# A bank for each half of the last accumulator, an earlier low part of the bias table, and weight splits that start one block later

## The chip, the cores and the metric

The kernel runs on one core of a Trainium2 chip. The metric is the device time of one execution in microseconds (us); the median of three runs of the kernel before is 1035.03 us. The core has a matrix engine (PE, whose weight loads the profile lists as PEld), a vector engine (DVE), a scalar engine (ACT), a general engine (POOL) and a queue engine (SP) that issues most transfers. Matmuls write their sums to PSUM, a memory of eight banks; a bank holds 512 float32 values in each of 128 partitions.

## The reference

One decoder layer for 256 tokens with 2048 features, in float32:

```
proj = x @ w_in                     # 16 latent queries, shared kv latent, gates, indexer, RG-LRU input
score = sum_h w_h * relu(q_idx_h . k_idx)        # causal, top 64 keys of each query
logits = q_lat . c_kv * scale + rel_bias[t5_bucket(t - s)]    # masked to the chosen keys
attn = softmax(logits) @ c_kv, up-projected per head, times silu(attn_gate), @ w_branch_a
h = RG-LRU(conv4(x_rnn)), times silu(rnn_gate), @ w_branch_b
merged = sigmoid(g_a) * attn_branch + sigmoid(g_b) * rnn_branch
out = layernorm(alpha * x + merged @ w_out) * ln_g + ln_b
```

## The kernel before, in words

Every weight is read once from memory, in pieces of 128x1024 float32 that the program numbers in the order of use. A piece lands in one of four `raw` buffers. ACT rounds it to a high part (`hi`, `hi_of`, line 97), DVE forms the low part (`lo`, `lo_of`, line 101) as raw minus hi, and PE multiplies with both, so that the sum has nearly float32 accuracy. There are five buffers for `hi` and five for `lo`. `split_to(n)` issues the split of all pieces up to n, `load_to(n)` their loads on SP.

The order of work on each engine is that in which the Python code records it; each engine takes its own instructions strictly in that order, and semaphores join the engines. The work has three stages that the change touches.

*The blocks* (lines 246 to 275). For k = 0 to 15, one block of x and one block of `wA` (kv latent, indexer key, half of the indexer queries) is split into `xs`, `ahi`, `alo` (three buffers each for `ahi` and `alo`), and PE adds 14 matmuls to six accumulators: `psc` (lines 266 to 268) and `psq` (line 204). In iteration k the split of block k + 1 is recorded first, then the matmuls of block k, and from k = 12 on one split of the main stream of weights (pieces 0 to 3).

*The main stream* (lines 779 to 818). Column jobs (`qi`, `ag`, `q`, `ga`, ...) follow each other on PE. Time is counted in ticks; a tick is one quarter of a small job's matmuls (8 of them). Side work is written as Python generators in an agenda: `spawn(t, gen)` starts one at tick t, and a `yield n` inside it puts its next step n ticks later. `post_a` evacuates `psc` at tick 0 and transposes the indexer key on PE (`psk`, line 333) at tick 3. `post_qi` evacuates `psq`. `scores(i)`, spawned at tick 13 + 4i, multiplies the indexer queries with the keys into two PSUM banks (`pss`, lines 379 and 381), reads them with ACT one tick later (lines 386, 387) and with DVE two ticks later (line 390). `rel`, spawned at tick 25, builds the table of relative position bias: high and low part of `rel_bias` in `rb`, then a matmul with a one-hot matrix (`psrel`, line 434) at tick 33. The tiles `psq`, `psk`, `pss` and `psrel` all come from four PSUM banks that are taken in turn (`aux_tile`): a new tile takes the bank of the fourth tile before it, once that tile's last reader is done. `scores(5)` takes two banks at tick 33 just ahead of `psrel`, and so `psrel` takes the bank of `pss4_0`, whose last reader is line 390 of `scores(4)`, recorded at tick 31.

*The last column chunk* (lines 891 to 905). The output projection's last 512 columns are done for one half of the tokens (t = 0) and then for the other (t = 1). For t = 1 they are cut in two halves of 256 columns, each 48 matmuls (lines 774 to 776). `residual` (lines 828, 829) adds alpha times x and takes the statistics of a finished half; `normalise(t)` forms mean and root, and for each 512 columns two DVE instructions, centre (line 851) and finish (line 854), and a store (line 855 on SP; the columns 1024 to 1535 go over ACT and POOL, lines 860 to 870). `normalise(0)` is recorded ahead of the first `residual` of t = 1. The accumulators come from four other banks, again in turn (`acc_tile`).

Of the kernel before, what the change touches and what calls it, by code (L numbers as in the profile page):

```python
# [73 lines left out]
def layer(ctx, tc, ar, out):  # L74
# [7 lines left out]
    def pool(name, side=None, **kw):  # L82
        return tc.tile_pool(name=name, bufs=1, side=side, **kw)
# [12 lines left out]
    def hi_of(hi, src):  # L96
        nc.scalar.activation(hi, src, AF.Copy)  # L97

    def lo_of(lo, src, hi):

        nc.vector.tensor_sub(lo, src, f(hi))  # L101

    def acc_tile(name):
        return psum.tile([P, 512], F32, name=name, tag="acc", bufs=4)

    def aux_tile(name):
        return psum.tile([P, 512], F32, name=name, tag="aux", bufs=4)

    def slot(name, dt=F32R):
        return big.tile([P, 2 * T], dt, name=name, tag="slot", bufs=16)  # L110
# [13 lines left out]
    def tick(t):  # L124
        for gen in agenda.pop(t, []):
            try:
                wait = next(gen)
            except StopIteration:
                continue
            spawn(t + (wait or 1), gen)  # L130
# [35 lines left out]
    def load_to(n):  # L166
        while st["load"] < min(n, len(halves)):
            i = st["load"]
            kind, a, s = halves[i]
            raw = wpool.tile([P, 1024], F32, name=f"raw{i}", tag="raw", bufs=4)  # L170
            if kind == "wt":
                src = ar["wt"][a, :, s * 8:(s + 1) * 8, :].rearrange("p k c -> p (k c)")
            else:
                src = ar[kind][a, s].rearrange("p k c -> p (k c)")
            nc.sync.dma_start(raw, src)
            raws[i] = raw
            st["load"] += 1

    def split_to(n):
        while st["split"] < min(n, len(halves)):  # L180
            i = st["split"]
            load_to(i + 1)
            raw = raws.pop(i)
            if NO + 24 <= i < NO + 28:
                pieces = []
                for e in range(2):
                    hi, lo = slot(f"wh{i}_{e}"), slot(f"wl{i}_{e}")
                    c = raw[:, e * 512:(e + 1) * 512]
                    hi_of(hi, c)
                    lo_of(lo, c, hi)  # L190
                    pieces.append((hi, lo))
                parts[i] = pieces
            else:
                hi = wpool.tile([P, 1024], F32R, name=f"hi{i}", tag="hi", bufs=5)
                lo = wpool.tile([P, 1024], F32R, name=f"lo{i}", tag="lo", bufs=5)
                hi_of(hi, raw)
                lo_of(lo, raw, hi)
                parts[i] = (hi, lo)
            st["split"] += 1

    def mm(ps, w, rhs, high, start, stop):

        n = 2 * T if high else T
        nc.tensor.matmul(ps[:, :n], w, rhs[:, :n], start=start, stop=stop)  # L204
# [16 lines left out]
    with pool("pha", side="right") as pha:  # L221
        ins = {}

        def load_a(k):
            xr = pha.tile([P, T], F32, name=f"xr{k}", tag="xr", bufs=4)
            nc.sync.dma_start(xr, ar["xT"][k])
            wr = pha.tile([P, NA], F32, name=f"wr{k}", tag="wr", bufs=4)
            if k == 0:
                nc.scalar.dma_start(wr[:, :A_Q], ar["wA"][k][:, :A_Q])
                nc.sync.dma_start(wr[:, A_Q:], ar["wA"][k][:, A_Q:])  # L230
            else:
                nc.sync.dma_start(wr, ar["wA"][k])
            ins[k] = (xr, wr)

        def split_a(k):
            xr, wr = ins.pop(k)
            hi_of(xs[:, k, :T], xr)
            lo_of(xs[:, k, T:], xr, xs[:, k, :T])
            hi = pha.tile([P, NA], F32R, name=f"ahi{k}", tag="ahi", bufs=3)
            lo = pha.tile([P, NA], F32R, name=f"alo{k}", tag="alo", bufs=3)  # L240
            for c in ([slice(0, A_Q), slice(A_Q, NA)] if k < 3 else [slice(0, NA)]):
                hi_of(hi[:, c], wr[:, c])
                lo_of(lo[:, c], wr[:, c], hi[:, c])
            return hi, lo

        for k in range(4):
            load_a(k)
        smalls = [(params, ar["params"]), (causal, ar["causal"]), (kvg, ar["kvg"].to_broadcast([P, DL])),
                  (relb, ar["relb"])]
        sp = {0: split_a(0)}  # L250
        for k in range(KT):
            if k + 1 < KT:
                sp[k + 1] = split_a(k + 1)
            if k + 4 < KT:
                load_a(k + 4)
            else:
                load_to(st["load"] + 1)
            if 8 <= k < 12:
                nc.sync.dma_start(*smalls[k - 8])
            hi, lo = sp.pop(k)  # L260
            fl = (k == 0, k == KT - 1)
            for t in range(2):
                o = psc[t][:, :A_Q]
                x_hi = xs[:, k, t * P:(t + 1) * P]
                x_lo = xs[:, k, T + t * P:T + (t + 1) * P]
                nc.tensor.matmul(o, x_hi, hi[:, :A_Q], start=fl[0], stop=False)
                nc.tensor.matmul(o, x_hi, lo[:, :A_Q], start=False, stop=False)
                nc.tensor.matmul(o, x_lo, hi[:, :A_Q], start=False, stop=fl[1])
            last = k == KT - 1
            for high in (False, True) if last else (True, False):  # L270
                for i in range(4):
                    w = (hi if high else lo)[:, A_Q + i * P:A_Q + (i + 1) * P]
                    mm(psq[i], w, xs[:, k, :], high, fl[0] and high, last and high)
            if k >= 12:
                split_to(k - 11)

    def evac(ps, name, dst=None):

# [145 lines left out]
    def rel():  # L424
        oh = idx.tile([32, VL], F32R, name="oh")
        nc.gpsimd.dma_start(oh, ar["onehot"])
        rb = idx.tile([32, 2, NH], F32R, name="rb")
        hi_of(rb[:, 0, :], relb)
        yield 6
        lo_of(rb[:, 1, :], relb, rb[:, 0, :])  # L430
        yield 2
        ps = aux_tile("psrel")
        for e in range(2):
            nc.tensor.matmul(ps[:NH, :], rb[:, e, :], oh, start=e == 0, stop=e == 1)
        yield
        v = idx.tile([NH, VL], F32, name="vrel")
        nc.scalar.activation(v, ps[:NH, :], AF.Copy, scale=DL ** 0.5)
        yield
        nc.gpsimd.dma_start(dv, v)
        for g in range(NH // HG):  # L440
            nc.gpsimd.dma_start(dz[g], bass.AP(tensor=dv.tensor, offset=dv.offset + g * SLAB,
                                               ap=[[0, P], [1, SLAB]]).rearrange("p (h v) -> p h v", h=HG))
            yield 10
# [303 lines left out]
    for i in range(4):  # L747
        spawn(1 + i, post_qi(i, psq[i]))
    spawn(25, rel())
    spawn(D0 + 20, lru_consts())  # L750
    for i in range(8):
# [17 lines left out]
    def products(o, w, i, d, xd, t, c=slice(0, 512)):  # L769

        hi, lo = (p[:, c] for p in (w[i] if isinstance(w, list) else [p[:, i * 512:(i + 1) * 512] for p in w]))
        mh = xd[:, t * P:(t + 1) * P]
        ml = xd[:, T + t * P:T + (t + 1) * P]
        nc.tensor.matmul(o, mh, hi, start=d == 0, stop=False)  # L774
        nc.tensor.matmul(o, mh, lo, start=False, stop=False)  # L775
        nc.tensor.matmul(o, ml, hi, start=False, stop=d == KT - 1)  # L776


    for kind, i in jobs:
        rhs = us if kind in ("ba", "bb") else {k: xs[:, k, :] for k in range(KT)}  # L780
        chunk = kind in CHUNKS
        ps = [acc_tile(f"ps_{kind}{i}_{t}") for t in range(2)] if chunk else acc_tile(f"ps_{kind}{i}")
        for qt in range(ticks((kind, i))):
            t = at[kind, i] + qt
# [12 lines left out]
            if t == FIN:  # L797
                dec_stack.close()
                fin = ctx.enter_context(pool("fin", side="right"))
                y = [fin.tile([P, DM], F32, name=f"y{e}") for e in range(2)]  # L800
# [5 lines left out]
            else:  # L806
                high = qt in (0, 3)
                w = parts[t // 2][0 if high else 1]
                for kk in range(8):
                    k = qt // 2 * 8 + kk  # L810
# [27 lines left out]
    rows = []  # L838
# [52 lines left out]
    last = range(NO + 24, NO + 32)  # L891
    cuts = [[slice(0, 512)], [slice(0, 256), slice(256, 512)]]
    for t in range(2):
        ps = acc_tile(f"psz{t}")
        for e, c in enumerate(cuts[t]):
            for n in last:
                for i in range(2):
                    d = 2 * (n - NO - 24) + i
                    products(ps[:, c], parts[n], i, d, xs[:, d, :], t, c)
                tick(t0)  # L900
                t0 += 1
                split_to(len(halves))
            residual(t, slice(3 * 512 + c.start, 3 * 512 + c.stop), 3 + e, ps[:, c])
        rows[-len(cuts[t]):] = [(t, slice(3 * 512, 4 * 512), ps if t else y[t][:, 3 * 512:])]
        normalise(t, 3 + len(cuts[t]))
    assert not agenda, agenda

# [51 lines left out]
```

## Time and profile before

| | |
|---|---|
| median of three runs (lowest, highest) | 1035.03 us (1034.36, 1035.72) |
| the profiled execution | 1034.45 us |
| its span, first to last instruction | 1032.7 us |
| PE busy | 1015.0 us, 98% of the span |
| PE weight loads busy | 881.0 us, 85% |
| DVE, ACT, POOL busy | 678.8 us (66%), 551.6 us (53%), 82.0 us (8%) |
| chain that ended last | PE 96%, DVE 2%, DMA 1% |
| mean granted PE clock | 0.995 of full |

A row of a timeline gives the start and length of an instruction (or of several alike, with their count), its engine, line and operation, the tile written and the tiles read, and in brackets how long the engine had sat idle before and what, by the profile, ended that. A matmul's length includes the time through the array, so that starts of neighbours lie closer together than a length.

### The profile page before, as it was taken

Reading aid. Unit: us, or ns where it says so; the run is one execution under the profiler, and the core shown is the slowest. Engines: PE = TensorE matmul, PEld = TensorE weight load, DVE = VectorE, ACT = ScalarE, POOL = GpSimd, SP = SyncE. Lnnn points to the kernel's source line nnn. Section 1 sums busy time; section 2 is a strip of 40 time slices with the busy share of each in tenths; the row PEclk is TensorE's granted clock in tenths of the full one; section 3 lists DMA queues with packets and bytes.
Section 4 is the critical chain, followed back from the end, with each engine's and each line's share of the span. In section 5 each row is a group of like instructions: output and inputs, shape, how many; then the busy total and the mean of one; then the engine's idle time right before and its main releaser. Section 6 shows DMA issues by size and latency. Waiting matters only on the chain.

```text
span 1032.7 us, 14867 instructions
## 1 busy us (share of the span) xinstructions
PE 1015.0 (98%) x5464; PEld 881.0 (85%) x5464; DVE 678.8 (66%) x1147; ACT 551.6 (53%) x910; POOL 82.0 (8%) x120
## 2 busy tenths in 40 slices
PE   9999999999999999999999999999999999999994
PEld 8888888998999988888888888888888888888884
DVE  6668775677677766544454888855577875566565
ACT  6666654555555565444334566588655554444431
POOL 0004312001111100000000000000500000000002
PEclk9999999999999999999999999999999999999997
DMA  9745877656566565665667666556666678666632
GB/s 306 265 144 171 276 252 233 194 171 178 170 189 174 183 184 162 185 191 196 192 196 213 196 186 194 171 183 190 193 190 185 200 252 283 186 192 190 186 120 82
DMA packets 61000, 201.41 MB, mean 195 GB/s; under 512 B 6608, under 2 KB 13136, under 8 KB 59904
## 3 DMA queue, kind: packets, MB, share of 16 engines
q1 hardware_dynamic: 59264, 191.29, 60.1%
q0 software_dynamic: 1232, 8.49, 2.1%
q8 instruction: 43, 0.70, 0.3%
q10 hardware_dynamic: 432, 0.70, 0.2%
q14 instruction: 29, 0.24, 0.1%
HBM read 198.31 MB, written 6.32 MB: 198 GB/s over the span
## 4 chain that ended last, share of the span: by engine, by line
PE 96%; DVE 2%; DMA 1%; issue 0%; ACT 0%; SPq 0%; DVEq 0%; ACTq 0%
PE ps_q L204 17%; PE ps_ag L204 9%; PE ps_rg L204 9%; PE ps_xr L204 9%; PE ps_ga L776 3%; PE ps_bb L776 3%; PE ps_gb L776 3%; PE ps_gb L775 3%; PE ps_ga L774 3%; PE ps_bb L774 3%; PE ps_ba L776 3%; PE ps_ba L774 3%; PE ps_bb L775 3%; PE ps_ga L775 3%; PE ps_gb L774 3%; PE ps_ba L775 3%
## 5 line engine op out<-in xcount | busy, mean ns | idle before, releaser
L101 DVE TENSOR_TENSOR lo<-raw,hi 128x1024 fp32r<-128x1024 f32 x324 | 399.5, 1234 | 307.1 <-ACT hi L97 303.3
L97 ACT ACTIVATE hi<-raw 128x1024 fp32r<-128x1024 f32 x324 | 341.5, 1054 | 175.6 <-PE ps_ba L776 52.6
L204 PE MATMUL ps_q<-xs,hi 128*128 128x512 f32 x512 | 122.4, 391 | 0.0
L204 PEld LDWEIGHTS ps_q<-xs,hi 128*128 128x128 f32 x512 | 94.0, 188 | 18.3
L204 PE MATMUL ps_q<-xs,lo 128*128 128x256 f32 x512 | 71.2, 283 | 0.0
L204 PEld LDWEIGHTS ps_q<-xs,lo 128*128 128x128 f32 x512 | 66.3, 190 | 1.4
L204 PE MATMUL ps_ag<-xs,hi 128*128 128x512 f32 x256 | 61.2, 391 | 0.0
L204 PE MATMUL ps_rg<-xs,hi 128*128 128x512 f32 x256 | 61.2, 391 | 0.0
L204 PE MATMUL ps_xr<-xs,hi 128*128 128x512 f32 x256 | 61.2, 391 | 0.0
L204 PEld LDWEIGHTS ps_rg<-xs,hi 128*128 128x128 f32 x256 | 47.1, 188 | 9.1
L204 PEld LDWEIGHTS ps_ag<-xs,hi 128*128 128x128 f32 x256 | 47.1, 188 | 9.1
L204 PEld LDWEIGHTS ps_xr<-xs,hi 128*128 128x128 f32 x256 | 47.0, 188 | 9.1
L774 PE MATMUL ps_bb<-hi,ub 128*128 128x512 f32 x128 | 50.4, 393 | 0.0
L774 PE MATMUL ps_ga<-hi,xs 128*128 128x512 f32 x128 | 50.0, 391 | 0.0
L776 PE MATMUL ps_bb<-hi,ub 128*128 128x512 f32 x128 | 49.9, 390 | 0.0
L776 PE MATMUL ps_ga<-hi,xs 128*128 128x512 f32 x128 | 49.9, 390 | 0.0
L776 PE MATMUL ps_gb<-hi,xs 128*128 128x512 f32 x128 | 49.9, 390 | 0.0
L775 PE MATMUL ps_gb<-lo,xs 128*128 128x512 f32 x128 | 49.8, 389 | 0.0
L775 PE MATMUL ps_ga<-lo,xs 128*128 128x512 f32 x128 | 49.8, 389 | 0.0
L775 PE MATMUL ps_bb<-lo,ub 128*128 128x512 f32 x128 | 49.8, 389 | 0.0
L774 PE MATMUL ps_ba<-hi,ua 128*128 128x512 f32 x128 | 49.8, 389 | 0.0
L775 PE MATMUL ps_ba<-lo,ua 128*128 128x512 f32 x128 | 49.8, 389 | 0.0
(273 smaller groups left out, 1888.7 us busy)
## 6 DMA issues: line engine op xcount, KB each, us to landing
raw<-in_wt SPq DMA_DIRECT2D x168, 512.0 KB, 4.2
raw<-in_wga SPq DMA_DIRECT2D x32, 512.0 KB, 3.6
raw<-in_wba SPq DMA_DIRECT2D x32, 512.0 KB, 3.5
raw<-in_wgb SPq DMA_DIRECT2D x32, 512.0 KB, 3.5
raw<-in_wbb SPq DMA_DIRECT2D x32, 512.0 KB, 3.7
raw<-in_wo SPq DMA_DIRECT2D x32, 512.0 KB, 3.6
wr<-in_wA SPq DMA_DIRECT2D x15, 424.0 KB, 4.6
dz<-dv POOLq DMA_DIRECT2D x4, 1024.0 KB, 8.6
```

The source lines that it names most:

```text
L97: nc.scalar.activation(hi, src, AF.Copy)
L101: nc.vector.tensor_sub(lo, src, f(hi))
L204: nc.tensor.matmul(ps[:, :n], w, rhs[:, :n], start=start, stop=stop)
L774: nc.tensor.matmul(o, mh, hi, start=d == 0, stop=False)
L775: nc.tensor.matmul(o, mh, lo, start=False, stop=False)
L776: nc.tensor.matmul(o, ml, hi, start=False, stop=d == KT - 1)
```

## The change

Three edits. The last accumulator of t = 1 becomes two tiles, one per half, and the line that joined the two halves for `normalise` goes, so that centre, finish and store are done per half of 256 columns. In `rel` the low part of `rb` is recorded at tick 28 where it was at tick 31; the matmul stays at tick 33. In the blocks, the splits of pieces 0, 1 and 2 are recorded in iterations 13, 14 and 15 where they were in 12, 13 and 14, and the split of piece 3 moves out of the blocks to tick 0 of the main stream, where `split_to(5)` issues it together with piece 4.

```diff
-            if k >= 12:
-                split_to(k - 11)
+            if k >= 13:
+                split_to(k - 12)
...
         hi_of(rb[:, 0, :], relb)
-        yield 6
+        yield 3
         lo_of(rb[:, 1, :], relb, rb[:, 0, :])
-        yield 2
+        yield 5
...
     for t in range(2):
-        ps = acc_tile(f"psz{t}")
         for e, c in enumerate(cuts[t]):
+            ps = acc_tile(f"psz{t}_{e}")
             for n in last:
...
             residual(t, slice(3 * 512 + c.start, 3 * 512 + c.stop), 3 + e, ps[:, c])
-        rows[-len(cuts[t]):] = [(t, slice(3 * 512, 4 * 512), ps if t else y[t][:, 3 * 512:])]
         normalise(t, 3 + len(cuts[t]))
```

ACT at the end of the blocks, before: `ahi` is a block's high part, `hi` a piece of the main stream, `pa0` the evacuated `psc`.

```order
L97 ACTIVATE ahi13_464<-wr13_395 128x848
L97 ACTIVATE hi0_484<-raw0_468 128x1024
L97 ACTIVATE xs_93<-xr14_418 128x256
L97 ACTIVATE ahi14_490<-wr14_420 128x848
L97 ACTIVATE hi1_510<-raw1_494 128x1024
L97 ACTIVATE xs_93<-xr15_443 128x256
L97 ACTIVATE ahi15_516<-wr15_445 128x848
L97 ACTIVATE hi2_536<-raw2_520 128x1024
L97 ACTIVATE hi3_556<-raw3_540 128x1024
L323 ACTIVATE pa0_585<-psc0_132 128x336
L97 ACTIVATE hi4_593<-raw4_591 128x1024
```

The same place in the changed kernel:

```order
L97 ACTIVATE ahi13_464<-wr13_395 128x848
L97 ACTIVATE xs_93<-xr14_418 128x256
L97 ACTIVATE ahi14_486<-wr14_420 128x848
L97 ACTIVATE hi0_506<-raw0_468 128x1024
L97 ACTIVATE xs_93<-xr15_443 128x256
L97 ACTIVATE ahi15_512<-wr15_445 128x848
L97 ACTIVATE hi1_532<-raw1_490 128x1024
L97 ACTIVATE hi2_552<-raw2_516 128x1024
L323 ACTIVATE pa0_581<-psc0_132 128x336
L97 ACTIVATE hi3_587<-raw3_536 128x1024
L97 ACTIVATE hi4_593<-raw4_591 128x1024
```

Block 14 now stands ahead of piece 0, and piece 3 behind `pa0`; the low parts stand on DVE in the same new order.

DVE around the low part of `rb`, before, with `lo18` to `lo20` pieces of the main stream and `rl4_0`, `rl4_1` the reads of `pss4_0` and `pss4_1`:

```order
L101 TENSOR_TENSOR lo18_1107<-raw18_959,hi18_1106 128x1024
L400 SCALAR_TENSOR_TENSOR score0_568<-rl3_0_1066,wi_567,score0_568 128x128
L400 SCALAR_TENSOR_TENSOR score1_569<-rl3_0_1066,wi_567,score1_569 128x256
L284 TENSOR_TENSOR s_ag2_1130<-ps_ag2_1015,r_ag2_1104 128x256
L400 SCALAR_TENSOR_TENSOR score0_568<-rl3_1_1069,wi_567,score0_568 128x128
L400 SCALAR_TENSOR_TENSOR score1_569<-rl3_1_1069,wi_567,score1_569 128x256
L101 TENSOR_TENSOR lo19_1150<-raw19_1002,hi19_1149 128x1024
L101 TENSOR_TENSOR rb_1044<-relb_90,rb_1044 32x16
L390 TENSOR_TENSOR rl4_0_1140<-pss4_0_1120,rl4_0_1140 128x128
```

The same place in the changed kernel:

```order
L101 TENSOR_TENSOR rb_1044<-relb_90,rb_1044 32x16
L101 TENSOR_TENSOR lo18_1108<-raw18_959,hi18_1107 128x1024
L400 SCALAR_TENSOR_TENSOR score0_564<-rl3_0_1066,wi_563,score0_564 128x128
L400 SCALAR_TENSOR_TENSOR score1_565<-rl3_0_1066,wi_563,score1_565 128x256
L284 TENSOR_TENSOR s_ag2_1131<-ps_ag2_1015,r_ag2_1105 128x256
L400 SCALAR_TENSOR_TENSOR score0_564<-rl3_1_1069,wi_563,score0_564 128x128
L400 SCALAR_TENSOR_TENSOR score1_565<-rl3_1_1069,wi_563,score1_565 128x256
L101 TENSOR_TENSOR lo19_1151<-raw19_1002,hi19_1150 128x1024
L390 TENSOR_TENSOR rl4_0_1141<-pss4_0_1121,rl4_0_1141 128x128
```

Only `rb` has moved; `lo19` and the read of `pss4_0` follow each other as before.

PE between the two halves of the last accumulator, before; a row names the engine whose semaphore it waits for:

```order
L775 MATMUL psz1_9810<-lo327_9725,xs_93 128x256
L776 MATMUL psz1_9810<-hi327_9724,xs_93 128x256
L774 MATMUL psz1_9810<-wh320_0_9624,xs_93 128x256 [waits DVE_49]
L775 MATMUL psz1_9810<-wl320_0_9625,xs_93 128x256
L776 MATMUL psz1_9810<-wh320_0_9624,xs_93 128x256
```

The same place in the changed kernel:

```order
L775 MATMUL psz1_0_9810<-lo327_9725,xs_93 128x256
L776 MATMUL psz1_0_9810<-hi327_9724,xs_93 128x256
L774 MATMUL psz1_1_9861<-wh320_0_9624,xs_93 128x256
L775 MATMUL psz1_1_9861<-wl320_0_9625,xs_93 128x256
L776 MATMUL psz1_1_9861<-wh320_0_9624,xs_93 128x256
```

The second half has a tile of its own and its first matmul has no wait for DVE.

## Rows read from the trace of the kernel before

**Rows 1.** Waits of PE in the whole span: us in total, times, longest
```profile
PE psz L774 <- DVE st L829: 4.8, 1, 4.8
PE psrel L434 <- ACT hi L97: 1.3, 1, 1.3
...
PE psc L267 <- DVE alo L101: 0.4, 1, 0.4
```

**Rows 2.** Timeline, the two halves of the last accumulator: start us, us, engine
```profile
1010.03 0.28 PE L776 MATMUL psz<-hi,xs 128*128 128x256 f32 x1
...
1014.67 0.43 DVE L829 BATCH_NORM_STATS2 st<-psz 128x6 f32<-128x256 f32 x1
...
1015.16 0.39 PE L774 MATMUL psz<-wh,xs 128*128 128x256 f32 x1 [4.85 <-DVE st L829]
...
1022.38 0.28 PE L776 MATMUL psz<-hi,xs 128*128 128x256 f32 x1
1022.70 0.43 DVE L828 SCALAR_TENSOR_TENSOR psz<-y,psz 128x256 f32<-128x256 f32 x1 [7.59 <-PE psz L776]
```

**Rows 3.** Stretches there: length, busy us (count) PE, PEld, DVE, ACT, POOL, clock, DMA
```profile
1004.40:1010.30 5.90, 5.90 (x49) 5.70 (x47) 4.70 (x10) 2.48 (x4) 1.29 (x1) 1.00 0.01 3
...
1015.10:1018.70 3.60, 3.54 (x18) 3.54 (x19) 0.01 (x1) 0.00 (x0) 0.00 (x0) 0.56 0.19 73
```

**Rows 4.** Timeline, the last instruction on DVE and the last store
```profile
1028.39 0.75 DVE L854 SCALAR_TENSOR_TENSOR y<-psz,lt,gb 128x512 f32<-128x512 f32 x1
1029.17 0.33 SPq L855 DMA_DIRECT2D out<-y  x1
```

**Rows 5.** Transfers by line: count, size of one, median us from issue to landing
```profile
xr<-in_xT SPq DMA_DIRECT2D x16, 128.0 KB, 4.5
...
out<-y SPq DMA_DIRECT2D x6, 256.0 KB, 2.1
```

**Rows 6.** Stretches of blocks 13, 14 and 15 on PE, columns as in Rows 3
```profile
35.68:38.01 2.33, 2.33 (x16) 2.15 (x15) 1.88 (x3) 2.33 (x4) 0.00 (x0) 1.00 0.78 311
38.01:40.97 2.96, 2.59 (x17) 2.18 (x15) 2.96 (x4) 2.82 (x5) 0.00 (x0) 1.00 0.64 197
40.97:43.40 2.43, 2.43 (x16) 2.17 (x15) 2.37 (x3) 0.45 (x1) 0.00 (x0) 1.00 0.66 226
```

**Rows 7.** Timeline, piece 0 on ACT, and block 14 on DVE and PE
```profile
35.04 1.06 ACT L97 ACTIVATE hi<-raw 128x1024 fp32r<-128x1024 f32 x1 [3.37 <-DMA raw<-in_wt]
...
37.61 1.03 DVE L101 TENSOR_TENSOR alo<-wr,ahi 128x848 fp32r<-128x848 f32 x1
...
38.70 0.42 PE L267 MATMUL psc<-alo,xs 128*128 128x336 f32 x1 [0.37 <-DVE alo L101]
```

**Rows 8.** Timeline, the first read of psq on DVE, and psk on PE and ACT
```profile
46.18 0.42 DVE L284 TENSOR_TENSOR s_qi<-psq,r_qi 128x256 f32<-128x256 f32 x1
...
49.00 0.38 PE L333 MATMUL psk<-ident,kd 128*128 128x128 f32 x2
...
49.41 0.39 ACT L97 ACTIVATE ks<-psk 128x256 fp32r<-128x256 f32 x1 [1.30 <-PE psk L333]
```

**Rows 9.** Costliest groups of the page: a low part, its count, busy us, mean ns
```profile
L101 DVE TENSOR_TENSOR lo<-raw,hi 128x1024 fp32r<-128x1024 f32 x324 | 399.5, 1234 | 307.1 <-ACT hi L97 303.3
```

**Rows 10.** Longest waits of ACT, then of DVE, between 50 and 96.5 us
```profile
ACT qis L97 <- DVE s_qi L284: 9.6, 5, 3.4
...
DVE lo L101 <- ACT hi L97: 12.3, 8, 3.6
```

**Rows 11.** Timeline around psrel
```profile
96.27 0.16 DVE L101 TENSOR_TENSOR rb<-relb,rb 32x16 fp32r<-32x16 f32 x1
96.36 0.27 DVE L390 TENSOR_TENSOR rl<-pss,rl 128x128 f32<-128x128 f32 x1
...
96.73 0.63 PE L434 MATMUL psrel<-oh,rb 32*16 32x512 f32 x2 [1.29 <-ACT hi L97]
```

**Rows 12.** Waits of the whole span, a piece's high part on ACT
```profile
ACT hi L97 <- PE ps_ba L776: 52.6, 32, 1.7
```

## The prediction, made before the changed kernel ran

> **What bounds the kernel now.** I read the waits of PE first. PE is busy for 98% of the span, so a stretch of it costs time one for one, and what can be won by order alone is what PE waits. The table [rows 1] shows three waits that the edits touch: 4.8 us for a statistic on DVE at the last accumulator, 1.3 us at psrel, 0.4 us for a block's low part. The question for each is what PE meets next once the named cause is gone, so I went to the timeline around each [rows 2, 7, 11], then to the stretches [rows 3, 6], where the cost of a wait can be read in another way: how long a piece of PE work of known size took beside its undisturbed neighbour.
>
> **Edit 1, a bank for each half.** The first half's last matmul starts at 1010.03. The second half's first starts at 1015.16, after DVE's statistic at 1014.67 [rows 2], because both halves are one tile and DVE still reads it. DVE is late because residual of the first half stands behind all of normalise(0). The undisturbed pitch of these matmuls is 5.90 us / 49 = 0.120 us [rows 3], so without the wait the second half would start at 1010.15: 5.01 us sooner. There is a second price. In the stretch after the wait the granted clock averages 0.56, mostly the lower level of 1.2 GHz, and only 18 matmuls fit into 3.60 us; before the wait it was 1.00, the level of 2.4 GHz, with PE busy throughout [rows 3]. From 1015.16 to the last start at 1022.38 the second half took 7.22 us; at 0.120 us its 47 intervals take 5.64 us, which is 1.58 us less. In the changed kernel the second half has a bank of its own and no wait for DVE, PE goes on without a gap, and I take it that the clock stays at its upper level as it did through the first half. Then the last start is at 1010.15 + 5.64 = 1015.79. DVE follows the last start by 0.32 us (1022.38 to 1022.70), so it starts the second residual at 1016.11 where it was 1022.70: **6.59 us gained**. Next in line is DVE itself: its statistic of the first half ends at 1014.67 + 0.43 = 1015.10, 1.0 us ahead. That is the slack; beyond it a slower normalise(0) would eat the gain.
>
> Behind that the tail is the same chain, with one step longer and one shorter. Centre and finish of the last 512 columns become two pairs of 256. A 512-wide one takes 0.75 us [rows 4], a 256-wide one on the same tile 0.43 [rows 2]: 4 x 0.43 - 2 x 0.75 = 0.22 us more on DVE, nothing beside it. The last store then carries 128 KB, not 256 KB; its issue follows DVE's end by 0.03 us as before [rows 4], and the store of the first 256 columns has been issued by then, hidden behind the second pair. No 128 KB store is in the trace. From one side it lands like a 256 KB one, after 2.1 us; the far bound is a 128 KB load among other loads, 4.5 us [rows 5], which would cost 2.4 us; from the other side, if the time to land went with the bytes alone, it would save 1.05 us. At the end nothing else is in the queues, so I stay by the row of the stores and take 0.1 us less. Tail: **0.1 us lost** (-0.8 to +2.6).
>
> The Trainium skill (VectorE: DVE Perf Modes, the section on the TRN2 errata) speaks against the split: an instruction pays a fixed latency, 120 cycles at 0.96 GHz for a PSUM source, and then one cycle per element. By that the two extra instructions cost 2 x 0.125 = 0.25 us, an estimate from the skill; the rows give 0.22, so rule and rows differ by less than I can measure. On the store the skill (DMA: Bandwidth & Descriptors, Anatomy of one DMA) has, fitted to transfers that GpSimd issues, a fixed part of about 2.0 us plus bytes over 436 GB/s. By that half the bytes save 0.30 us, an estimate, and the tail would come out even; the trace has no such store.
>
> **Edit 2, the low part of the bias table.** PE waits 1.3 us at psrel, and the instruction that moves ends just before psrel starts. But psrel takes the bank of pss4_0, and the last reader of that bank is the first of the two DVE reads of line 390: 96.36 + 0.27 = 96.63, and psrel starts at 96.73 [rows 11]. The moved one ended at 96.43 and would have let psrel go 0.2 us sooner. The name in brackets (ACT) is inferred; ACT's read of that bank was a tick earlier. So the wait stays; what goes is the moved instruction's place ahead of the read, 96.36 - 96.27: **0.09 us gained**. At its new place it delays piece 18's low part by the same 0.09 us, hidden behind DVE's wait for POOL there; if that cover were gone, the gain would be nothing.
>
> **Edit 3, splits one block later.** ACT reaches piece 0 long before its data: it sits idle 3.37 us for the load and starts at 35.04 [rows 7]. Block 14's high part stands behind it, its low part comes at 37.61 on DVE, and PE stops in block 14 at 38.70 [rows 7]. Block 13 took 2.33 us, block 14 took 2.96, block 15 took 2.43 [rows 6]: 0.63 + 0.10 = 0.73 us lost, more than the 0.4 in the table of waits, since a matmul's modelled length hides part. In the new order block 14 is split in that idle time. Its buffers are those of block 11, which PE leaves one block before 35.68, at 33.35, so its low part is ready near 35.4 and PE asks for it at 38.2. Block 15 follows piece 0 on ACT and takes the slot that block 14 has now, ready at 37.61 + 1.03 = 38.64 for a use near 40.5. **0.73 us gained**, and the main stream starts at 42.67.
>
> What pays is the stretch behind: piece 3's split moves behind the evacuation of psc. High part 1.06 us [rows 7], low part 1.23 [rows 9]. On DVE it pushes the first read of psq from 46.18 to about 46.6 by my count of the queue (pa at 42.9, high part to 44.3, two low parts to 46.7), ending at 47.0. psk takes that bank at 49.00 - 0.73 = 48.27 [rows 8]: 1.2 us to spare. ACT has 1.30 us idle before ks [rows 8], which takes the extra 1.06 us less the 0.73 that all moves up. Piece 3 is first used by PE near 51, its low part is done near 45.5, and load 7, which waits for its buffer, goes out 2.1 us later for a use near 57.
>
> Does the gain reach psrel? From ks to psrel ACT and DVE hardly rest, and the waits between 50 and 96.5 are for each other or for POOL, none for PE [rows 10]: one serial chain that begins at psk. psk moves up 0.73 us, ks with it, so the chain and the read that frees pss4_0 do too.
>
> **The sum.** 0.73 + 0.09 + 6.59 - 0.1 = 7.3 us. The profiled execution took 1034.45 us, so 1027.15. It lies 0.58 us under the median of the three runs; from the median, 1035.03 - 7.3 = **1027.7 us**.
>
> **Rivals.**
> - *The psrel wait goes as well.* For it: it is in the table and the moved instruction is next to it. Against: the bank's reader is later still. Another 1.2 us: 1026.5.
> - *The head gain is swallowed at psrel.* For it: the chain from ks to psrel is serial, and if the extra pair makes ks start late by 0.73 us, PE waits that much longer at psrel. Against: 1.30 us of idle on ACT. 1028.4.
> - *The clock falls anyway in the second half.* For it: it fell at that place. Against: it fell after a wait that is gone. All 48 at 3.60 / 18 = 0.2 us end near 1019.9, gaining about 2.8 us, not 6.6: 1031.5.
> - *The second half still waits* (the change does not do what it says). Only if its bank were held; it takes that of the fourth accumulator before it, read long ago. 0.7 us gained: 1034.3.
> - *Slower: the splits lose their lead.* Every later pair is queued behind the displaced one, so PE could begin to wait at each piece. It decides from 9.4 us / 324 pairs = 0.03 us a pair; at 0.05 us it is 16 us, 1044. Against: high parts wait for PE to free buffers, 52.6 us in all in one job kind alone [rows 12], and ACT and DVE are idle for a third of the span or more.
>
> **Numbers.** Forecast 66%, psrel goes 7%, head swallowed 13%, clock 6%, still waits 4%, splits 4%. The range from 1025.9 to 1029.6 holds the first three with the scatter of 0.7 us that the runs show around their median and a store a little slower or faster than I took; the far bound of the store stays out with the 14% of the last three. No change within 0.2% (2.07 us, about what a measurement of this kernel can tell) is the case of the second half that still waits, 4%; slower 4%; faster 92%.
>
> **What would show it.** Right: no wait of PE at psz and a full clock to its end; the second residual on DVE some 6.6 us nearer to the end of the first half; blocks 14 and 15 at 2.33 us; the wait at psrel still near 1.2 us, with the same DVE read ahead of it. Wrong: a wait at psrel of 0.2 us or of 2, a granted clock under 1 in the second half, PE waiting for a low part between 43 and 60 us, or a last store that takes well over 2.2 us to land.

## The result, and the profile after

The changed kernel takes 1028.6 us (median of four runs, 1028.06 to 1030.81); the kernel before, in the same comparison, 1034.69 us. The ratio is 0.9939, with a 95% interval of 0.9921 to 0.9956. The forecast was 1027.7 us with a range of 1025.9 to 1029.6: right in sign and inside the range, 0.9 us too low. The profiled execution took 1028.45 us with a span of 1026.7 us, against 1034.45 and 1032.7.

First the waits of PE in the whole span, which answer to [rows 1]:

```profile
PE psrel L434 <- ACT hi L97: 2.0, 1, 2.0
PE warm L217 <- DVE eps L139: 1.0, 1, 1.0
PE psc L266 <- ACT ahi L97: 0.8, 1, 0.8
```

The 4.8 us at psz and the 0.4 us at block 14 are gone. The wait at psrel has grown from 1.3 to 2.0 us, and one of 0.8 us in the first block is new. The timeline of the last accumulator, against [rows 2]:

```profile
1014.73 0.42 DVE L828 SCALAR_TENSOR_TENSOR psz<-y,psz 128x256 f32<-128x256 f32 x1
1015.19 0.43 DVE L829 BATCH_NORM_STATS2 st<-psz 128x6 f32<-128x256 f32 x1
...
1016.27 0.28 PE L776 MATMUL psz<-hi,xs 128*128 128x256 f32 x1
...
1016.59 0.43 DVE L828 SCALAR_TENSOR_TENSOR psz<-y,psz 128x256 f32<-128x256 f32 x1 [0.97 <-PE psz L776]
```

And the stretches of its two halves, columns as in [rows 3]:

```profile
1004.85:1010.75 5.90, 5.90 (x50) 5.87 (x49) 4.67 (x10) 2.46 (x4) 1.29 (x1) 1.00 0.01 3
1010.75:1016.50 5.75, 5.75 (x49) 5.60 (x47) 4.76 (x7) 0.46 (x1) 1.53 (x1) 1.00 0.48 182
```

PE runs through both halves at one pitch with the clock at 1.00. From the first residual to the second, DVE needs 1016.59 - 1014.73 = 1.86 us. The first residual in the timeline of the kernel before:

```profile
1014.22 0.42 DVE L828 SCALAR_TENSOR_TENSOR psz<-y,psz 128x256 f32<-128x256 f32 x1
```

So there it was 1022.70 [rows 2] - 1014.22 = 8.48. Edit 1 is worth 6.62 us between these two executions. The timeline of the very end, against [rows 4]:

```profile
1021.50 0.48 DVE L851 SCALAR_TENSOR_TENSOR psz<-psz,mv,gb 128x256 f32<-128x256 f32 x1
1022.02 0.48 DVE L854 SCALAR_TENSOR_TENSOR y<-psz,lt,gb 128x256 f32<-128x256 f32 x1
1022.42 0.48 DVE L851 SCALAR_TENSOR_TENSOR psz<-psz,mv,gb 128x256 f32<-128x256 f32 x1
1022.94 0.48 DVE L854 SCALAR_TENSOR_TENSOR y<-psz,lt,gb 128x256 f32<-128x256 f32 x1
1023.45 0.33 SPq L855 DMA_DIRECT2D out<-y  x1
```

The stores on SP by size, columns as in [rows 5]:

```profile
out<-y SPq DMA_DIRECT2D x5, 256.0 KB, 2.1
...
out<-y SPq DMA_DIRECT2D x2, 128.0 KB, 2.2
```

From the second residual to DVE's last end it is 6.83 us, where it was 6.44; from the last store's issue to the end of the span 3.25 us, where it was 3.53. The 2.2 is the middle of two stores: the last one lands 1.9 us after its issue, where the last one before took 2.2, and the one ahead of it takes longer. Together the tail is 0.11 us longer.

In the head, the stretches of blocks 13, 14 and 15, against [rows 6]:

```profile
36.23:38.56 2.33, 2.33 (x16) 2.15 (x15) 2.33 (x3) 2.33 (x4) 0.00 (x0) 1.00 0.87 294
38.56:40.89 2.33, 2.33 (x16) 2.14 (x15) 2.33 (x3) 0.58 (x1) 0.00 (x0) 1.00 0.68 232
40.89:43.22 2.33, 2.33 (x17) 2.16 (x15) 0.06 (x1) 0.00 (x0) 0.00 (x0) 1.00 0.71 248
```

And the timeline where the gain is lost, against [rows 8] and [rows 11]:

```profile
43.42 0.45 ACT L323 ACTIVATE pa<-psc 128x336 f32<-128x336 f32 x1 [4.27 <-PE psq L204]
...
48.83 0.38 PE L333 MATMUL psk<-ident,kd 128*128 128x128 f32 x2
...
49.25 0.39 ACT L97 ACTIVATE ks<-psk 128x256 fp32r<-128x256 f32 x1 [0.37 <-PE psk L333]
49.42 0.87 DVE L101 TENSOR_TENSOR qis<-s_qi,qis 64x256 fp32r<-64x256 f32 x2
50.32 0.42 ACT L339 ACTIVATE junk<-pa 128x256 f32<-128x256 f32 x1 [0.69 <-DVE qis L101]
...
96.85 0.48 DVE L390 TENSOR_TENSOR rl<-pss,rl 128x128 f32<-128x128 f32 x2
97.23 0.62 PE L434 MATMUL psrel<-oh,rb 32*16 32x512 f32 x2 [1.96 <-ACT hi L97]
```

All three blocks take 2.33 us, so edit 3 did its work. They lie 0.56 us later than in the kernel before, since PE waited 0.80 us in the first block: the second block's weights landed later, and ACT could begin their high part only at 7.32 us, where it was 6.75.

Behind `ks` ACT now stands still for 0.69 us before the first `junk` instruction, which in the kernel before followed `ks` at once, the low part of `qis` being done on DVE by 49.53. The timeline of the kernel before:

```profile
48.66 0.87 DVE L101 TENSOR_TENSOR qis<-s_qi,qis 64x256 fp32r<-64x256 f32 x2
...
49.82 0.42 ACT L339 ACTIVATE junk<-pa 128x256 f32<-128x256 f32 x1
```

The `junk` tile shares three buffers with the `s` tiles, and this one is free only when DVE has formed the low part of the first `qis`.

So the two profiled executions differ by +0.51 us up to the first residual (psrel itself is 0.50 us later than in [rows 11]), -6.62 us between the residuals, +0.11 us in the tail: -6.00 us, which is 1028.45 - 1034.45.

### The profile page after: what moved, and what is told of

It reads as the page before. It is cut to its first block, busy times and chain, and to the rows that moved or that the text cites. A ratio compares the mean times of both kernels' runs of the same rounds, so it can differ in the third digit from the quotient of the medians.

```text
span 1026.7 us, 14870 instructions
## 1 busy us (share of the span) xinstructions
PE 1012.7 (99%) x5464; PEld 878.9 (86%) x5464; DVE 679.9 (66%) x1149; ACT 551.5 (54%) x910; POOL 82.1 (8%) x120
## 4 chain that ended last, share of the span: by engine, by line
PE 98%; DVE 1%; DMA 1%; ACT 0%; SPq 0%; issue 0%; ACTq 0%
PE ps_q L204 17%; PE ps_ag L204 9%; PE ps_rg L204 9%; PE ps_xr L204 9%; PE ps_ga L774 3%; PE ps_gb L776 3%; PE ps_bb L776 3%; PE ps_bb L774 3%; PE ps_ga L775 3%; PE ps_ga L776 3%; PE ps_ba L775 3%; PE ps_ba L774 3%; PE ps_bb L775 3%; PE ps_gb L774 3%; PE ps_gb L775 3%; PE ps_ba L776 3%
```

## The experiments

Ratios are to runs of the kernel before on the same chip, with 95% intervals.

**One edit at a time**, on the kernel before. Their diffs are the three hunks of the change, each by itself.

Edit 1 alone: 

> The kernel before with edit 1 alone (the own bank for each of the last three accumulators). Theory A (nearly all of the change is edit 1): PE's wait of 4.8 us at psz is gone, the granted clock after it stays at 1.00, and the median is 6.2 to 6.8 us below the kernel before, equal to the changed kernel within 0.4 us. Theory B (the head of the program gives its 0.8 us as well, and the start of the profiled run of the changed kernel hid it): 5.5 to 6.0 us below before, and so 0.6 to 0.8 us above the changed kernel.

Edit 2 alone: 

> The kernel before with edit 2 alone (low part of the bias table three ticks sooner). Theory A (psrel waits for the addition that reads the bank, not for the table): the wait at psrel goes from 1.29 to about 1.2 us and the total is the same within 0.3 us. Theory B (the table was what it waited for): the wait is gone, and the total is 1.3 us below before.

Edit 3 alone: 

> The kernel before with edit 3 alone (first splits one block later). Theory A (the gain is taken back at psrel): blocks 14 and 15 take 2.33 us each and ACT copies psc 0.7 us sooner than before, measured from the end of block 13; the first junk tile then waits on ACT for the low part of the first qis, and PE's wait at psrel grows from 1.3 to about 2.0 us, so that psrel starts within 0.15 us of where it did, measured from the end of block 13, and the total is the same within 0.3 us. Theory B (the gain carries through): the psrel wait stays at 1.3 us, and the total is 0.7 us below before.

Measured: edit 1 1028.01 us, ratio 0.9931 (0.9918 to 0.9943); edit 2 1035.54 us, 1.0001 (0.9992 to 1.0010); edit 3 1036.46 us, 1.0011 (1.0002 to 1.0020); the kernel before 1035.3 us (21 runs, 1033.8 to 1036.59). The waits came out as theory A says on all three (but for the one at psrel with edit 2, which stayed at 1.30 where 1.2 was expected), with two misses in size: edit 1 gave 7.3 us, more than the 6.2 to 6.8 expected, and edit 3 came out 1.2 us slower, not the same within 0.3. The profiled run of edit 3 alone is 2.65 us longer than that of the kernel before (spans 1035.33 and 1032.67), and two stretches at the lower level of the clock hold that. The first stands behind the psz wait, columns as in [rows 3]:

```profile
1016.70:1022.60 5.90, 5.87 (x27) 5.87 (x28) 0.00 (x0) 0.00 (x0) 0.00 (x0) 0.50 0.12 44
1022.65:1025.30 2.65, 2.65 (x22) 2.46 (x21) 0.00 (x0) 0.00 (x0) 0.00 (x0) 1.00 0.00 0
```

Here 27 matmuls ran at the lower level of the clock, against at most 18 in [rows 3]. From residual to residual it took 9.56 us, against 8.48 before and 8.41 with edit 2 alone. Nothing in edit 3 touches this place, so the length of the low stretch changes from run to run, and with it the price of the wait: 6.6 us in one execution, 7.7 in another.

The second stands behind the wait at psrel, which edit 3 lengthens from 1.29 to 1.97 us. The same window with edit 3 alone and then in the kernel before:

```profile
97.60:101.00 3.40, 3.40 (x13) 3.01 (x13) 2.20 (x7) 1.77 (x3) 1.80 (x3) 0.50 0.76 250
...
97.60:101.00 3.40, 3.40 (x20) 2.95 (x19) 2.19 (x7) 1.87 (x4) 1.77 (x3) 1.00 0.84 254
```

From psrel (96.75 us) to the first residual (1015.79) this run takes 919.04 us, against 917.49 before: 1.55 us more, beside the 1.08 in the tail. So the clock can fall behind the longer wait, and then that wait costs far more than its length. It does not always: of the profiled executions it fell there in one of the three with a wait of 1.96 or 1.97 us, and in none of the four with 1.3. How often it falls in the runs without a profile is not shown.

The head can be compared free of the start's luck by measuring psrel from the moment at which ACT copies `psc` (line 323), us:

| kernel | block 13 starts | psc copied | psrel starts | from psc to psrel | wait at psrel |
|---|---|---|---|---|---|
| before | 35.68 | 43.60 | 96.73 | 53.13 | 1.29 |
| edit 1 alone | 36.09 | 43.78 | 96.91 | 53.13 | 1.29 |
| edit 2 alone | 36.32 | 43.89 | 97.03 | 53.14 | 1.30 |
| edit 3 alone | 35.74 | 42.92 | 96.75 | 53.83 | 1.97 |
| all three | 36.24 | 43.42 | 97.23 | 53.81 | 1.96 |
| all three, junk tiles apart | 35.81 | 42.98 | 95.98 | 53.00 | 1.14 |

Edit 3 stretches the way from `psc` to psrel by 0.7 us. Ahead of `psc` its gain depends on the start. With it, block 13 to `psc` takes 7.18 us; the kernel before takes 7.92, but edits 1 and 2 alone, which started late, take 7.69 and 7.57, since a later PE waits less for block 14's low part (with edit 2 alone that begins 0.29 us later, PE's block 13 0.64 later). So edit 3 wins 0.7 us after an early start and 0.4 to 0.5 after a late one, and loses 0.7 in both cases. The changed kernel, which started late, therefore reaches psrel 0.32 us later than edit 1 alone (97.23 against 96.91), of which only 0.15 is the start, and its span is longer by no more than that (1026.67 against 1026.34). Edit 2 moves nothing.

**The wait without the standing engine** (kernel before). The line that adds the matmuls stands ahead of the second half:

```diff
+            if t == 1 and e == 1:
+                fill = acc_tile("fill")
+                for j in range(21):
+                    nc.tensor.matmul(fill, xs[:, 0, :P], parts[NO + 31][0][:, :512], start=j == 0, stop=j == 20)
```

> The kernel before with 21 matmuls of 512 columns into a bank that nothing reads, put between the first and the second half of the last accumulator, so that PE works through the wait for the bank instead of standing; the order and the wait stay. Their result is not used. Theory A (the median of before holds two prices, 5.0 us for the wait and some 2.3 us for a low clock after it, whose length differs from run to run): the clock stays at 1.00 behind the fillers, the median is 1032.7 to 1033.3 us, 2.0 to 2.6 us below before and 5 us above the kernel with edit 1 alone, and the runs lie within 1.5 us of one another. Theory B (the low clock comes from something else in the tail, not from the standing engine): the clock is 0.5 to 0.6 behind the fillers too, and the median is that of before.

Measured: 1033.61 us (1032.79 to 1035.19), ratio 0.9982 (0.9973 to 0.9991). The timeline on PE, the fillers and the start of the second half:

```profile
1010.52 4.95 PE L899 MATMUL fill<-hi,xs 128*128 128x512 f32 x21
1015.56 0.39 PE L774 MATMUL psz<-wh,xs 128*128 128x256 f32 x1
```

The stretch of the second half, columns as in [rows 3]:

```profile
1015.60:1021.30 5.70, 5.70 (x47) 5.70 (x48) 0.00 (x0) 0.00 (x0) 0.00 (x0) 1.00 0.11 43
```

Theory A holds in its mechanism: with PE at work the clock stays at 1.00, and from residual to residual it takes 7.00 us instead of 8.48, so the low clock cost that execution of the kernel before 1.48 us and the wait 7.00 - 1.86 = 5.14. In the medians the low clock is worth 1.6 us where 2.0 to 2.6 was expected, the median is 0.3 us above the expected range, and the runs spread over 2.4 us, not 1.5. What makes that spread the one profile does not show.

**Junk tiles with buffers of their own** (changed kernel):

```diff
-            junk = tmp_tile(f"junk{t}", "s")
+            junk = tmp_tile(f"junk{t}", "j", 2)
```

> The changed kernel with buffers of their own for the two junk tiles, which then share none with the s tiles. Theory A (the junk tile's wait for the low part of the first qis is what takes edit 3's gain on its way to psrel): ACT's 0.69 us of idle before the junk instruction are gone, the wait at psrel falls from 2.0 to about 1.3 us, and the median is 0.5 to 0.8 us below the changed kernel, 1027.9 us or, without the start's extra wait of 0.6 us, 1027.3. Theory B (ACT has slack behind the junk instructions, and VectorE's own queue, with one more split pair in it, is what is late): the wait at psrel stays at 1.9 to 2.0 us.

Measured: 1027.35 us, ratio 0.9919 (0.9906 to 0.9933). The timeline on ACT behind `psk`:

```profile
48.81 0.38 ACT L97 ACTIVATE ks<-psk 128x256 fp32r<-128x256 f32 x1 [0.37 <-PE psk L333]
49.21 0.42 ACT L339 ACTIVATE junk<-pa 128x256 f32<-128x256 f32 x1
```

The waits of PE in the whole span:

```profile
PE psrel L434 <- ACT hi L97: 1.1, 1, 1.1
PE warm L217 <- DVE eps L139: 1.0, 1, 1.0
```

The idle time is gone and psrel comes 0.8 us sooner behind `psc`: the shared buffer was what took edit 3's gain.

**psrel taken out of the ring** (changed kernel): ten ticks later, behind the last scores; the same without edit 3; and two ticks later only.

```diff
         lo_of(rb[:, 1, :], relb, rb[:, 0, :])
-        yield 5
+        yield 15
```

> The changed kernel with the psrel matmuls ten ticks later, behind the last of the scores, where they take another bank of the ring. Theory A (psrel's place in the ring is what takes the head's gain): the wait of 2.0 us at psrel is gone and no score matmul waits in its place, since each then takes a bank that was read a round earlier; 1.7 to 2.0 us below the changed kernel, about 1026.7 us. Theory B (VectorE and ScalarE are behind in this stretch as a whole, and the wait only moves): a wait of 1 us or more turns up at a later score or split, and the total falls by less than 1.0 us.

Measured: 1025.93 us (1025.77 to 1026.12), ratio 0.9910 (0.9897 to 0.9924). This is the fastest version. Its span is 1024.1 us, and of PE's waits only the one at the start is left:

```profile
PE warm L217 <- DVE eps L139: 1.0, 1, 1.0
```

Theory A holds. What psrel feeds, the first load of a bias on SP, is issued at 164.1 us (164.8 in the changed kernel), so ten ticks near 100 us cost nothing there. The gain over the changed kernel, 2.7 us by the medians, is more than the 1.7 to 2.0 expected. Between the two profiled executions it is 2.56: the wait of 1.96 and a `psc` 0.58 us sooner (42.84 against 43.42), all of that from an earlier start (block 13 at 35.66 against 36.24).

Without edit 3 (and with the same late psrel): 

> The changed kernel with psrel ten ticks later and with edit 3 taken back (first splits at block 12 again). Theory A (edit 3 saves PE 0.7 us in blocks 14 and 15, and the wait at psrel took that back): with no wait at psrel the saving counts in full, so this kernel is 0.6 to 0.9 us slower than the one with psrel late and edit 3 in, 1026.6 to 1026.8 us. Theory B (edit 3 is worth nothing, the start's luck made the blocks look shorter): the same within 0.2 us, 1025.9 us.

Measured: 1026.81 us, ratio 0.9914 (0.9900 to 0.9927). Its `psc` is copied at 43.78 us, against 42.84 in the version with edit 3, and the spans are 1025.0 and 1024.1 us. From `psc` to the end both take 981.2 to 981.3 us, so behind a psrel that waits for nothing every gain ahead of `psc` counts in full. But only part of it is edit 3's here: this run had waited 0.90 us in its first block and began block 13 0.64 us later (36.30 against 35.66), and from there to `psc` it took 7.48 us against 7.18, so that edit 3 is worth 0.3 us between these two executions. The medians, 0.9 us apart, are as theory A has them, but the ratios overlap and the starts of the other runs are not known; the size of the gain in the median is not shown.

Two ticks later (`yield 7`): 

> The changed kernel with psrel two ticks later instead of ten, so that it still stands between two groups of scores in the ring of banks. Theory A (it is the ring: a score of the next group then takes the bank that was read last): the wait at psrel is gone, but the second score matmul of the next group waits 0.7 to 1.1 us for the addition that reads its bank, and the median lies 0.7 to 1.1 us above the kernel with psrel ten ticks later, at 1026.6 to 1027.1 us. Theory B (two ticks give the additions all the time they need): no wait, and the same within 0.2 us as ten ticks, 1025.9 us.

Measured: 1027.71 us, ratio 0.9919 (0.9905 to 0.9932). In the timeline the wait has moved to the second score tile of the next group:

```profile
101.09 0.28 PE L379 MATMUL pss<-ks,qis 128*128 128x256 f32 x1
102.19 0.48 DVE L390 TENSOR_TENSOR rl<-pss,rl 128x128 f32<-128x128 f32 x2
...
102.62 0.36 PE L379 MATMUL pss<-ks,qis 128*128 128x256 f32 x1 [1.01 <-DVE rl L390]
```

It waits 1.01 us for the addition that reads its bank, as theory A has it; a psrel in the midst of the scores turns the ring by one bank, and someone has to take the bank that was read last. By the ratios this costs 0.9 us against ten ticks; the median itself lies higher than expected, as do the runs of the kernel before beside it (1036.12 us).

**The last 512 columns joined again** (on the kernel with psrel ten ticks later):

```diff
-        to = ps if t else y[t][:, c]
+        to = ps if t and e < 3 else y[t][:, c]
...
+        rows[-len(cuts[t]):] = [(t, slice(3 * 512, 4 * 512), y[t][:, 3 * 512:])]
         normalise(t, 3 + len(cuts[t]))
```

> The kernel with psrel ten ticks later, with the two last residuals written to the y tile, so that centring, finishing and the store of the last 512 columns are one step again instead of two. Theory A (the split costs VectorE 0.4 us and saves the last store 0.3 us): from the second residual to the end of VectorE's last instruction 6.4 us instead of 6.8, from the last store's issue to the end of the span 3.5 us instead of 3.25, total 0.0 to 0.2 us lower. Theory B (the smaller last store is worth more than the two extra steps): 0.2 us or more slower.

Measured: 1026.51 us, ratio 0.9912 (0.9898 to 0.9926), 0.6 us slower by the medians, where the ratios overlap. It has the sign of theory B and only part of its reason. The store did what A said (3.5 us from its issue to the end), but the timeline shows a centre that ran long:

```profile
1017.66 0.75 DVE L851 SCALAR_TENSOR_TENSOR pso<-pso,mv,gb 128x512 f32<-128x512 f32 x1
...
1018.57 1.26 POOL L869 TENSOR_TENSOR y<-y,gb 128x512 f32<-128x512 f32 x1 [0.83 <-ACT y L868]
1019.12 1.27 DVE L851 SCALAR_TENSOR_TENSOR y<-y,mv,gb 128x512 f32<-128x512 f32 x1
```

Reading its tensor from `y` beside POOL it took 1.27 us; from PSUM it takes 0.75. That 0.52 us outweighs the extra steps it saves: from the second residual to DVE's last end it is 6.96 us, not 6.4, against 6.84 with the split. Of the 0.56 us between the two profiled executions 0.12 lie there, 0.27 in the store and 0.17 ahead of `psc`, where this run started later.

**The changed kernel again.** 

> The changed kernel once more. Theory A (edits 2 and 3 together move nothing that reaches the end): the median is that of edit 1 alone, 1027.6 to 1028.5 us, the wait at psrel is 1.9 to 2.0 us, and psc is copied at 42.8 to 43.0 us where PE has no extra wait in the first block, at 43.4 where it has. Theory B (the changed kernel's first four runs were typical and the edits cost something): 1028.6 us or more, over 0.5 us above edit 1 alone.

Measured: 1029.88 us, ratio 0.9936 (0.9924 to 0.9949), beside a kernel before of 1036.12 us. The wait at psrel is 1.96 us and `psc` is copied at 43.20 after an extra wait of 0.5 us. By the ratio it stands with edit 1 alone (0.9931), so edits 2 and 3 together move nothing that the ratios can tell; the median alone would speak for theory B. The profiled run took 1028.23 us and the other four 1029.64 to 1029.99; where their 1.6 us lie no profile shows. A low clock behind the longer wait at psrel, which cost 1.55 us with edit 3 alone, is one candidate. In the first four runs the one of 1030.81 us had a mean granted clock of 0.993 where the others had 0.997 and 0.998, which shows a longer time at the lower level but not its place. That stays open.

## Why the prediction was right, and where it was wrong

*Edit 1 was right in mechanism and, for the execution it was worked from, in size*: 6.59 us forecast, 6.62 found, the wait 5.01 against 5.14 and the clock 1.58 against 1.48. By medians edit 1 is worth 7.3 us. The clock term can be larger than in the execution I worked from (the step took 7.70 us with edit 3 alone), and I gave it no range; but the fillers put it at 1.6 us in the medians. With the 5.14 of the wait that makes 6.7, and some 0.5 us of the 7.3 have no shown cause.

*The tail came out even for two wrong reasons that cancel.* I took 0.43 us for a 256-wide centre or finish from the residual's row. These steps take 0.48: where the residual takes 0.69 us for 512 columns, they take 0.75 [rows 4], so the difference stood in the trace. Issued as dependent pairs, they cost 0.39 us more, not 0.22. The store gave back 0.28 us, not 0.1. The Trainium skill (DMA: Bandwidth & Descriptors, Anatomy of one DMA) puts a fixed part and a part by bytes on a transfer, from which I had estimated 0.30 us for half the bytes; the trace agrees, 3.53 against 3.25 us from issue to the end of the span.

*Edit 2*: the reading that psrel waits for the bank and not for the table was right. The 0.09 us was not gained. At its new place the instruction delays DVE's next `s_ag` addition (2.81 us behind the additions of line 390 with edit 2 alone, 2.73 before), and ACT's sigmoid, which stands ahead of its next high part, waits for that. The cover that I named was not there.

*Edit 3, up to psk, was right* for a start as early as that of the execution I worked from: 0.7 us, and `psk` and `ks` came that much sooner (`ks` 5.83 us behind `psc`, against 5.81).

*The step that failed* is "one serial chain that begins at psk. psk moves up 0.73 us, ks with it, so the chain and the read that frees pss4_0 do too". The chain also begins at the first `qis`. The pair of piece 3 delayed that low part on DVE from 5.06 to 6.00 us behind `psc`, and `junk` waits for its buffer. I followed the extra pair to the first read of `psq` and to the idle time before `ks`, and not to what stands behind `ks` on ACT. With separate junk buffers the idle time and the extra 0.7 us on the way to psrel are both gone, so this is shown. The rival "the head gain is swallowed at psrel", 13%, had the price right (1028.4) and the place wrong by one instruction: `ks` was not late, its successor was. Neither it nor the forecast held the price that edit 3 alone showed, a low clock behind the longer wait at psrel.

Worked from its own execution, the forecast was 1027.15 us, and the changed kernel's profiled execution took 1028.45. The 1.30 us between are 0.68 of edit 3, 0.09 of edit 2 and 0.56 of the later start, less 0.03 in the tail and edit 1. The start is a matter of the execution: block 13 begins at 35.66 to 35.86 us in six of the twelve profiled executions and at 36.02 to 36.36 in the other six, with versions that hold edit 3 and versions that do not in both groups, and the late load comes before anything that an edit moves.

That the median, 1028.6, lies within 0.9 us of 1027.7 is partly luck: edit 1 gave 0.7 us more by medians than the sum had for it, and edits 2 and 3 gave nothing where it had 0.82.

## What to carry to other kernels

A gain counts only up to the next wait, so follow the displaced work through every buffer it holds, shared names of scratch tiles among them, until the engine that sets the time has passed its next wait. A side job that borrows a bank from a ring turns the ring for all that follow; put it where the ring has slack, and check who gets the bank that was read last. A wait in front of a busy matrix engine is priced by its length and by the clock behind it, and the second part differs from run to run; once, with edit 3 alone, it came behind a wait of only 2 us.

## What the runs showed that was not expected

The low clock behind the psz wait had no fixed length: 27 matmuls in one profiled run, at most 18 in another, at the same place after the same 4.8 us. Without the wait, the runs of edit 1 alone lie within 1.1 us of one another, those of the kernel before beside them within 2.8. That wait is not the only source of such a spread: the changed kernel has none there, and its four runs lie 2.75 us apart.

A DVE step on two tensors in SBUF took 1.27 us beside a POOL step where 0.75 was usual. The Trainium skill (SBUF — State Buffer, Who interferes with whom) says that a DVE instruction with two SBUF inputs contends with a GpSimd (here POOL) instruction that reads SBUF, and one with at most one such input, outside the two-port modes, does not. The trace agrees: in the same run POOL's 1.27 us from 1016.48 on lay beside the finish of `pso`, whose tensor is in PSUM, and that took 0.75 us; the finish of `y` at 1020.42 read two tensors in SBUF with POOL idle, and took 0.75 as well. The kernel before had shown it, in `normalise(0)` with POOL at work from 1008.69 and from 1010.81:

```profile
1008.77 1.75 DVE L854 SCALAR_TENSOR_TENSOR y<-y,lt,gb 128x512 f32<-128x512 f32 x1
...
1011.22 1.63 DVE L854 SCALAR_TENSOR_TENSOR y<-y,lt,gb 128x512 f32<-128x512 f32 x1
```

The next one, at 1013.55, has no POOL step beside it and takes 0.75. These two stand ahead of the statistic that PE waited for, so by an estimate from these rows some 1.9 us of the wait at psz came from them (1.75 + 1.63 - 2 x 0.75); no run tested that.
